# Rotary embedding on one core: tile 0 in one load with the tables behind it, and loads 5 to 7 issued together after store 2

## The chip, the cores and the metric

The kernel runs on one core of a Trainium2 chip. The metric is the device time of one execution in microseconds, lower being better. A run's profile gives the span from the first to the last instruction; the execution's time is a little longer than this.

The core has five engines with queues of their own: PE (matrix products; PEld is its weight load), DVE and POOL (elementwise work), ACT (here used to copy results out of PSUM) and SP, which in this kernel issues every transfer between main memory and the on-chip memory. The transfers themselves are carried by 16 DMA engines. PSUM is the small memory that matrix products write to.

## The reference

```python
# x (16, 512, 1024) float32; cos, sin (512, 32) float32; num_heads 16
x = x.reshape(batch, seq, num_heads, head_dim)           # head_dim 64
x1, x2 = x[..., :32], x[..., 32:]
rotated = concatenate([x1 * cos - x2 * sin, x1 * sin + x2 * cos], axis=-1)
```

cos and sin depend on the position in the sequence alone, and are the same for all batches and heads. 33.5 MB are read and 33.5 MB written; each element costs two products and one sum.

## The kernel before, in words

**Tiles.** The batch is cut into eight tiles of two batches each (`NB = 2`, `NT = 8`). A tile lies on 128 partitions, 64 for each of its batches; a partition holds eight consecutive positions of the sequence (`KK = 8`) of 1024 numbers each, 32 KB, which are contiguous in main memory. A tile is 4 MB. One of the eight positions of a tile is called a row here; the work is done row by row, on 128 x 1024 numbers.

**Buffers.** The pool `xp` has five tile buffers (`BUFS = 5`). The result of a tile is written over its input, so that one buffer is loaded, computed in place, stored from, and can be loaded again only when its store has landed. Tiles 5, 6 and 7 use the buffers of tiles 0, 1 and 2. The pool `bp` has six buffers of one row (`B_BUFS = 6`) for POOL's products; the raw sin and cos tables are first loaded into two of them. Three PSUM buffers `ps` of one row hold the sums.

**Tables.** sin and cos (64 KB each) are loaded on 64 partitions, spread to 128 by PE (lines 104 and 105), and DVE then makes the signed table `sns` from sin (lines 107 and 108) and copies a piece of it to PSUM (line 111). POOL's first product needs `sns`, DVE's first product the cos table in PSUM.

**A row.** POOL multiplies the row, with the halves of each head swapped, by `sns` into `b` (line 155), in all rows but row 6. DVE multiplies the row by cos into `ps` (line 156). For rows 1, 4 and 6 (`PE_ROWS`), PE adds the swapped product to `ps` by a product with the identity (line 164), and ACT copies the sum back over the row (line 167). For the other rows DVE adds the two (line 145). In row 6 DVE makes the swapped product itself, in place (line 158).

**Order.** The schedule is written out by hand: each engine runs its instructions in the order of the program, and waits where the data or a buffer is not there yet. SP's queue is in the same order. SP issues the first two rows of tile 0, then sin and cos, then the rest of tile 0 in pieces of two rows (`FIRST = (2, 4, 6, 8)`, four pieces of 1 MB, each with 8 KB a partition), then tiles 1 to 4 whole (32 KB a partition). In the loop over tiles, SP issues the store of tile t when its last row is computed (line 76); the last tile is stored in two halves (`LAST_OUT`). After the stores of tiles 1, 2 and 3 it issues load 5, 6 and 7 respectively (line 72 by way of line 180): so load 5 follows store 1, load 6 store 2 and load 7 store 3. Load 5 waits on SP until store 0 has landed, load 6 until store 1, load 7 until store 2. Whatever stands behind a waiting transfer on SP's queue waits too.

Of the kernel before, what the change touches and what calls it, by code (L numbers as in the profile page):

```python
# [13 lines left out]
BUFS = 5  # L14
# [4 lines left out]

DVE_B = (6,)  # L20

FIRST = (2, 4, 6, 8)
LAST_OUT = (4, 8)


# [1 line left out]
def kernel(  # L27
# [21 lines left out]
    NT = batch // NB  # L49
# [18 lines left out]
    def load(t, lo=0, hi=KK):  # L68
        if tiles[t] is None:
            tiles[t] = xp.tile([P, F], FP32, name="xt")  # L70
        s = slice(lo * dim, hi * dim)
        nc.sync.dma_start(out=tiles[t][:, s], in_=x_v[t][:, s])  # L72

    def store(t, lo=0, hi=KK):
        s = slice(lo * dim, hi * dim)
        nc.sync.dma_start(out=out_v[t][:, s], in_=tiles[t][:, s])

    load(0, 0, FIRST[0])
    sin_sb = bp.tile([P, dim], FP32, name="b")[:PB, : KK * half]
    cos_sb = bp.tile([P, dim], FP32, name="b")[:PB, : KK * half]  # L80
    nc.sync.dma_start(out=sin_sb, in_=sin_v)
    nc.sync.dma_start(out=cos_sb, in_=cos_v)
    for lo, hi in zip(FIRST, FIRST[1:]):
        load(0, lo, hi)
# [28 lines left out]
    def cos_b(k):  # L113
        c = cos_t[:, k * half : (k + 1) * half]
        return bass.AP(tensor=c.tensor, offset=c.offset, ap=[c.ap[0], [0, 2 * nh], [1, half]])

    def over_heads(s):
        return bass.AP(tensor=s.tensor, offset=s.offset, ap=[s.ap[0], [0, nh], [1, hd]])

    def swapped(r, n):  # L120
        return bass.AP(
            tensor=r.tensor, offset=r.offset + half, ap=[r.ap[0], [hd, n], [-half, 2], [1, half]]
        )

    def swapped_signed(i):

        s = sns_t[:, i * hd : (i + 1) * hd]
        return bass.AP(
            tensor=s.tensor, offset=s.offset + half, ap=[s.ap[0], [0, nh], [-half, 2], [1, half]]
        )  # L130

    def pairs(r):
        return r.rearrange("p (a j) -> p a j", j=half)
# [4 lines left out]
    def halves(r):  # L138
        return r.rearrange("p (h a j) -> p h a j", a=2, j=half)
# [3 lines left out]
    def add():  # L143
        r, ps, b = pending.pop(0)
        nc.vector.tensor_tensor(out=r, in0=ps, in1=b, op=ALU.add)  # L145

    for t in range(NT):
        xt = tiles[t]
        for k in range(KK):
            r = xt[:, k * dim : (k + 1) * dim]  # L150
            ps = pr.tile([P, dim], FP32, name="ps")
            if k not in DVE_B:
                b = bp.tile([P, dim], FP32, name="b")
                sk = sns[:, k].rearrange("p a j -> p (a j)")
                nc.gpsimd.tensor_tensor(out=halves(b), in0=swapped(r, nh), in1=over_heads(sk), op=ALU.mult)  # L155
            nc.vector.tensor_tensor(out=pairs(ps), in0=pairs(r), in1=cos_b(k), op=ALU.mult)  # L156
            if k in DVE_B:
                nc.vector.tensor_tensor(  # L158
                    out=halves(r), in0=halves(r), in1=swapped_signed(DVE_B.index(k)), op=ALU.mult
                )  # L160
            if k in PE_ROWS:
                for c in range(0, dim, BANK):
                    rhs = swapped(r[:, c : c + BANK], BANK // hd) if k in DVE_B else b[:, c : c + BANK]
                    nc.tensor.matmul(  # L164
                        out=ps[:, c : c + BANK], lhsT=ident, rhs=rhs, start=False, stop=True, skip_group_check=True
                    )
                nc.scalar.copy(out=r, in_=ps)  # L167
            else:
                pending.append((r, ps, b))
            while len(pending) > (1 if k + 1 < KK else 0):  # L170
                add()
        if t < NT - 1:
            store(t)
        else:
            lo = 0
            for hi in LAST_OUT:
                store(t, lo, hi)
                lo = hi
        if t >= 1 and t + BUFS - 1 < NT:
            load(t + BUFS - 1)  # L180


# [33 lines left out]
```

## Time and profile before

| | us |
|---|---|
| median of 8 runs | 165.05 |
| lowest and highest of them | 163.71 and 165.37 |
| the profiled execution's own time | 163.71 |
| its span | 161.8 |
| DVE busy | 132.5 |
| POOL busy | 130.2 |
| PE busy | 85.9 |
| ACT busy | 25.6 |

Over the span the transfers move 67.26 MB, 416 GB/s on average. How to read the page: busy time is that of an engine's instructions; the slices cut the span in 40 equal parts and give the busy share of each in tenths, for DMA the mean over its 16 engines. In a timeline the first column is the start of a piece in us from the span's start, the second its length, then the engine, the line and the operation, what it writes and reads, and how many were merged. An SP line of a transfer is its issue; the time from there to its landing is asked separately.

| transfers | count | KB each | median us from issue to landing |
|---|---|---|---|
| loads of a whole tile | 7 | 4096 | 29.3 |
| stores of a whole tile | 7 | 4096 | 26.1 |
| pieces of tile 0 | 4 | 1024 | 7.5 |
| halves of the last store | 2 | 2048 | 12.8 |
| sin, cos | 1 each | 64 | 4.9, 4.6 |

### The profile page before, as it was taken

How to read it: one execution, taken by the hardware profiler on the slowest of the kernel's cores; microseconds unless marked ns; L12 is line 12 of the kernel's file. 1: busy time of each engine (PE TensorE's matmuls, PEld its weight loads, DVE VectorE, ACT ScalarE, POOL GpSimd, SP SyncE). 2: the span in 40 equal slices, each digit the busy share in tenths (PEclk: the TensorE clock that was granted, in tenths of full speed). 3: DMA queues.
4: the chain of work that ended last, by engine and by line, in shares of the span. 5: the costliest groups of instructions: out<-in, count | busy, mean ns of one | idle time of the engine just before them, and what ended most of it. 6: DMA issues, size and time to landing. Idle time of an engine off the chain costs nothing.

```text
span 161.8 us, 602 instructions
## 1 busy us (share of the span) xinstructions
PE 85.9 (53%) x106; PEld 27.2 (17%) x106; DVE 132.5 (82%) x118; ACT 25.6 (16%) x25; POOL 130.2 (80%) x62
## 2 busy tenths in 40 slices
PE   6405380763785288328732773857584628472000
PEld 1202020221221022102210220222022202220000
DVE  1097656999999999999999999999999999997000
ACT  0000502102211211220222022012202220222000
POOL 1079999999999999999999999999999999300000
PEclk9999959675558555955589555555555895579655
DMA  5999999999999999999999999999999999999992
GB/s 186 389 421 462 421 478 397 413 486 397 413 486 389 397 470 429 399 478 413 405 478 413 413 462 423 389 486 421 397 437 446 405 462 429 405 462 397 425 437 109
DMA packets 3042, 67.26 MB, mean 416 GB/s; under 512 B 352, under 2 KB 480, under 8 KB 480
## 3 DMA queue, kind: packets, MB, share of 16 engines
q1 hardware_dynamic: 3040, 67.24, 97.5%
q14 instruction: 2, 0.02, 0.0%
HBM read 33.69 MB, written 33.55 MB: 416 GB/s over the span
## 4 chain that ended last, share of the span: by engine, by line
DVE 51%; PE 15%; issue 10%; POOL 6%; ACT 4%; DMA 3%; DVEq 1%; SPq 0%; ACTq 0%; POOLq 0%
DVE ps L156 30%; DVE xt L145 16%; PE ps L164 14%; POOL b L155 6%; DVE xt L158 5%; ACT xt L167 4%; DMA b<-in_sin_dram 3%; DVEq L211 1%; PE tab L104 1%; PE tab L105 1%; DVE sns L107 0%; SPq L72 0%; DVE sns L108 0%; DVEq L156 0%; DVEq L145 0%
## 5 line engine op out<-in xcount | busy, mean ns | idle before, releaser
L155 POOL TENSOR_TENSOR b<-xt,sns 128x1024 f32<-128x1024 f32 x56 | 129.5, 2347 | 8.1 <-DVE sns L108 7.8
L156 DVE TENSOR_TENSOR ps<-xt,tab 128x1024 f32<-128x1024 f32 x64 | 76.8, 1226 | 7.1 <-ACT xt L167 6.1
L164 PE MATMUL ps<-b,ident 128*128 128x512 f32 x64 | 54.9, 1007 | 46.8 <-DVE ps L156 31.7
L145 DVE TENSOR_TENSOR xt<-ps,b 128x1024 f32<-128x1024 f32 x40 | 48.0, 1217 | 0.9 <-POOL b L155 0.9
L167 ACT COPY xt<-ps 128x1024 f32<-128x1024 f32 x24 | 24.3, 1012 | 104.6 <-PE ps L164 95.2
L164 PE MATMUL ps<-xt,ident 128*128 128x512 f32 x32 | 26.3, 969 | 10.6 <-DVE xt L158 6.9
L164 PEld LDWEIGHTS ps<-b,ident 128*128 128x128 f32 x64 | 16.9, 290 | 83.2 <-issue 51.5
L164 PEld LDWEIGHTS ps<-xt,ident 128*128 128x128 f32 x32 | 8.4, 290 | 30.0 <-DVE xt L158 17.5
L158 DVE TENSOR_TENSOR xt<-xt,tab 128x1024 f32<-128x1024 f32 x8 | 9.8, 1220 | 0.3
L107 DVE TENSOR_SCALAR sns<-tab 128x256 f32<-128x256 f32 x1 | 0.4, 425 | 6.6 <-PE tab L105 6.6
L167 ACT ACT_TABLE_LOAD x1 | 1.3, 1283 | 17.6 <-PE ps L164 17.6
L95 PE MATMUL ps<-zero 128*128 128x512 bf16 x6 | 2.7, 630 | 1.2 <-DVE zero L89 1.2
L104 PE MATMUL tab<-b,spread 64*128 64x256 f32 x2 | 1.2, 696 | 2.2 <-DMA b<-in_sin_dram 2.2
L95 PEld LDWEIGHTS <-zero 128*128 128x128 bf16 x6 | 0.7, 137 | 2.3 <-DVE zero L89 1.2
L105 PE MATMUL tab<-b,spread 64*128 64x256 f32 x2 | 1.1, 631 | 0.0
L104 PEld LDWEIGHTS tab<-b,spread 64*128 64x128 f32 x2 | 0.5, 307 | 3.1 <-issue 3.1
L89 DVE MEMSET zero<- 128x256 uint32 x1 | 0.3, 272 | 0.9 <-PEq L197 0.9
L105 PEld LDWEIGHTS tab<-b,spread 64*128 64x128 f32 x2 | 0.7, 333 | 0.2
L103 DVE COPY spread<-ident 64x64 f32<-64x64 f32 x2 | 0.3, 181 | 0.2 <-POOL ident masks.py:199 0.2
masks.py:197 POOL MEMSET ident<- 128x128 f32 x1 | 0.2, 204 | 0.3 <-POOLq L197 0.3
L108 DVE COPY sns<-tab 128x256 f32<-128x256 f32 x1 | 0.4, 415 | 0.0
masks.py:199 POOL TENSOR_SCALAR_AFFINE_SELECT ident<-ident 128x128 f32<-128x128 f32 x1 | 0.3, 292 | 0.1
(5 smaller groups left out, 0.6 us busy)
## 6 DMA issues: line engine op xcount, KB each, us to landing
xt<-in_x_dram SPq DMA_DIRECT2D x7, 4096.0 KB, 29.3
out_dram<-xt SPq DMA_DIRECT2D x7, 4096.0 KB, 26.1
xt<-in_x_dram SPq DMA_DIRECT2D x4, 1024.0 KB, 7.5
out_dram<-xt SPq DMA_DIRECT2D x2, 2048.0 KB, 12.8
b<-in_sin_dram SPq DMA_DIRECT2D x1, 64.0 KB, 4.9
b<-in_cos_dram SPq DMA_DIRECT2D x1, 64.0 KB, 4.6
```

What stands on the lines that cost most here:

```text
L95: nc.tensor.matmul(out=ps[:, c : c + BANK], lhsT=zero[:, :P], rhs=zero, start=True, stop=True)
L104: nc.tensor.matmul(out=sin_t, lhsT=spread, rhs=sin_sb, start=True, stop=True)
L105: nc.tensor.matmul(out=cos_t, lhsT=spread, rhs=cos_sb, start=True, stop=True)
L107: nc.vector.tensor_scalar_mul(out=sns[:, :, 0, :], in0=sin_k, scalar1=-1.0)
L108: nc.vector.tensor_copy(out=sns[:, :, 1, :], in_=sin_k)
L145: nc.vector.tensor_tensor(out=r, in0=ps, in1=b, op=ALU.add)
L155: nc.gpsimd.tensor_tensor(out=halves(b), in0=swapped(r, nh), in1=over_heads(sk), op=ALU.mult)
L156: nc.vector.tensor_tensor(out=pairs(ps), in0=pairs(r), in1=cos_b(k), op=ALU.mult)
L158: nc.vector.tensor_tensor(out=halves(r), in0=halves(r), in1=swapped_signed(DVE_B.index(k)), op=ALU.mult)
L164: nc.tensor.matmul(out=ps[:, c : c + BANK], lhsT=ident, rhs=rhs, start=False, stop=True, skip_group_check=True)
L167: nc.scalar.copy(out=r, in_=ps)
L211: with _tile.TileContext(nc) as tc:
```

## The change

```diff
-FIRST = (2, 4, 6, 8)
+FIRST = (8,)
 LAST_OUT = (4, 8)
@@
-        if t >= 1 and t + BUFS - 1 < NT:
-            load(t + BUFS - 1)
+        if t + 1 == NT - BUFS:
+            for n in range(BUFS, NT):
+                load(n)
```

The first edit makes tile 0 one transfer of 4 MB with 32 KB a partition. The code around it stays, `load(0, 0, FIRST[0])` ahead of the two tables and a loop over the remaining pieces behind them, which is now empty. SP's queue therefore begins with the whole of tile 0, then sin, cos, and tiles 1 to 4.

The second edit acts once, at t = 2: after store 2, SP issues loads 5, 6 and 7 one behind the other. The order on SP's queue is then store 0, store 1, store 2, load 5, load 6, load 7, store 3 and so on to store 7. What each load waits for (stores 0, 1 and 2) is the same as before. No instruction on PE, DVE, ACT or POOL is added, removed or moved.

## The prediction

> **What bounds the kernel now.** I read the page's slices and DMA totals first, since a kernel that moves 67 MB for three operations on each element is likely bound by its transfers.
>
> ```profile
> span 161.8 us, 602 instructions
> ...
> DMA  5999999999999999999999999999999999999992
> ...
> q1 hardware_dynamic: 3040, 67.24, 97.5%
> ```
>
> Between the first and the last slice the transfer engines are full: there is no hole. One queue, SP's, carries all of it. So the time is the transfers' bytes at their rate, plus a head and a tail, as long as SP always has the next transfer queued before the last one is through. That condition is what I check next, in the order of time on SP's queue.
>
> ```profile
> 0.73 0.37 SPq L72 DMA_DIRECT2D xt<-in_x_dram  x1
> 1.16 0.53 SPq L81 DMA_DIRECT2D b<-in_sin_dram  x1
> 1.74 0.58 SPq L82 DMA_DIRECT2D b<-in_cos_dram  x1
> 2.36 4.35 SPq L72 DMA_DIRECT2D xt<-in_x_dram  x7
> 32.61 16.87 SPq L76 DMA_DIRECT2D out_dram<-xt  x2
> 62.86 0.34 SPq L72 DMA_DIRECT2D xt<-in_x_dram  x1
> 65.97 0.33 SPq L76 DMA_DIRECT2D out_dram<-xt  x1
> 72.67 0.34 SPq L72 DMA_DIRECT2D xt<-in_x_dram  x1
> 82.80 0.33 SPq L76 DMA_DIRECT2D out_dram<-xt  x1
> 92.10 0.34 SPq L72 DMA_DIRECT2D xt<-in_x_dram  x1
> ```
>
> The reader is to see when each transfer is handed over (first column). The store of tile 0 goes out at 32.61, that of tile 1 at 49.14, that of tile 2 at 65.97; load 5 at 62.86, the moment store 0 has landed (its issue-to-landing time, asked alone, is 30.2, so 62.8), and load 6 at 72.67, when store 1 has landed (49.14 + 23.5 = 72.6). With the issue-to-landing time of each transfer asked one by one, the landings stand in a row: tile 0's four pieces at 5.8, 8.9, 11.4, 13.9; loads 1 to 4 at 23.6, 33.3, 43.0, 53.0; then store 0 62.8, store 1 72.6, load 5 82.3, store 2 92.0, load 6 101.9, the rest one after another to 160.6. Each 4 MB tile takes 9.7 to 10.2. When store 1 ends at 72.6, load 5 has waited since 62.9 and store 2 since 66.0: nine and six us of reserve.
>
> Where compute begins is set by the tables:
>
> ```profile
> 6.17 1.19 PE L104 MATMUL tab<-b,spread 64*128 64x256 f32 x2 [2.24 <-DMA b<-in_sin_dram]
> 7.16 1.06 PE L105 MATMUL tab<-b,spread 64*128 64x256 f32 x2
> 8.25 0.42 DVE L107 TENSOR_SCALAR sns<-tab 128x256 f32<-128x256 f32 x1 [6.63 <-PE tab L105]
> 8.59 0.41 DVE L108 COPY sns<-tab 128x256 f32<-128x256 f32 x1
> 9.09 2.35 POOL L155 TENSOR_TENSOR b<-xt,sns 128x1024 f32<-128x1024 f32 x1 [7.79 <-DVE sns L108]
> ```
>
> sin lands at 6.04 (1.16 + 4.88 in the chain of waits), and POOL's first product starts at 9.09: 3.05 later, all of it the chain through PE and DVE. From there POOL never waits for x again:
>
> ```profile
> L155 POOL TENSOR_TENSOR b<-xt,sns x56: 2334/2347/2369, 9.1 to 136.5; 128x1024 f32<-128x1024 f32 x56
> ...
>   DVE sns L108: 7.8, 1
> ```
>
> Its 56 products start 2.31 apart (127.4 over 55 steps); the one real wait is that for the tables. In tile 0 the rows are wanted at 9.1, 13.7, 18.3 and 23.0 in pairs and their pieces land at 5.8, 8.9, 11.4 and 13.9, so none of the pieces is late. The stores of tiles 0 to 4 go out 16.5 to 16.8 apart, set by DVE (14 operations of 1.14 to 1.25 a tile), 23.5 after POOL's start for the first. Compute is thus a rigid train: if its start moves by D, every store's issue moves by D.
>
> **What the Trainium skill says.** "DMA: Bandwidth & Descriptors", section Queues, rings and completion order: each DMA engine consumes the descriptors of a ring in ring order. The trace agrees as far as it goes: sin, issued behind the first 1 MB piece, lands 0.28 after it, at 6.04 against 5.76. The same page, section Latency and other measured facts, gives about 0.6 us to the first byte of such a transfer; here the first one is issued at 0.73 and the first packets show at 1.74, so I use the measured 1.0. "TensorE: Matmul & The Clock Gate", Part 1: an idle window of about 3.4 us puts the clock back to half. PE idles longer before the tables after the change; but the four table matmuls already start 0.43 apart, and 256 columns in float32 at L164's later pace (0.85 for 512 in stretches granted half clock) are the same 0.43. They run at half clock now, so there is no warmth to lose.
>
> **The change part by part.**
>
> *Tile 0 in one transfer, the tables behind it.* Three issues fall away. Packets of 8 KB took 0.309 to 0.319 us in the trace, those of 32 KB mostly 1.213, which is 0.303 for 8 KB. Each engine carries 32 of the small ones, so 32 x about 0.008 = 0.25 saved. The bytes of tile 0 and the tables are the same, and in before they are all landed at 13.9; now at 13.6. But the tables come last: cos at 13.6, sin 0.33 ahead of it (the two lie 0.33 apart in before) at 13.3 instead of 6.0. So D = 13.3 - 6.04 = 7.25. cos lies no later behind sin than before, and its matmuls follow sin's. The chain of 3.05 stays: POOL starts at 16.3. All of tile 0 is there by then, but no row of it was waited for before, so this gives nothing back. Loads 1 to 4 land 0.25 earlier, and are wanted 7.25 later. The stores now go out at 39.9, 56.4 and 73.2.
>
> *Loads 5, 6 and 7 behind store 2.* On SP's queue they stood behind stores 1, 2 and 3; now the order is store 0, store 1, store 2, loads 5, 6, 7, store 3. Load 5 no longer goes out at 62.9 but only after SP has finished its wait for tile 2's compute, at 73.2. Stores 0 and 1 land at 62.5 and 72.35 (before, less 0.25). From there to 73.2 nothing is queued at all: DMA stands still. The two parts meet here. With the old start, store 2 would be issued at 66.0, 6.4 ahead, and its reserve would cover; D of 7.25 eats that.
>
> *The hole.* Store 2 issued at 73.2, first packets 1.0 later at 74.2, its 4 MB in 9.7 and about 0.35 from the last packet's end to the landing (the last store of before: 160.30 and 160.63): landed at 84.3, against 72.35 + 9.75 = 82.1 without a hole: 2.2. What is not shown is how fast a store starts into idle engines. The one start shown, the first 1 MB piece, had packets of up to 1.04 in place of 0.31 and cost slow engines some 1.2. Bounds 0 and 1.2; I take 0.2, since the stretch at the head also holds the very first accesses of the run, which the later one does not. Hole: 2.4.
>
> *After the hole.* Loads 5 and 6 are issued straight behind store 2 (stores 0 and 1 have landed), 19.4 of transfers. Load 7 waits on SP for store 2 (84.5), with store 3 behind it; tile 3 is computed at 90.0, so nothing real is held up, and DMA has work to 104. Load 5 lands at 84.5 + 9.7 = 94.2; POOL wants tile 5 at 89.92 + 7.25 = 97.2: 3 us of cover, where before there were 7.6 (82.3 to 89.9). Load 6 at 104 against 113.4, load 7 at 114 against 129.6. The turn of direction: tiles whose successor is of the other kind took 10.03 (load 4), 9.90 (load 6), 10.18 (load 7), but 9.68 (load 5); loads 5 and 6 are now followed by loads. Bounds 0 and 0.5; I take 0.2 saved.
>
> *Sum.* Last landing: 160.63 - 0.25 + 2.4 - 0.2 = 162.6. Against that stands compute's own tail: the last store is issued at 148.55 + 7.25 = 155.8, and alone it would take 1.0 + 4.85 + 0.35, landing at 162.0. That is earlier, so the transfers still end last, by 0.6 only: before, that reserve was 5.9 (148.55 + 6.2 = 154.7). The span grows by 1.95 to about 163.8. The profiled execution took 163.71 for its span of 161.8, 1.9 around it; after, 165.65 on its scale. The median of the runs is 165.05, 1.3 above the profiled one, so I add the 1.95 there: **167.0**.
>
> **The rivals.**
>
> *A, the forecast:* the hole before store 2 decides; 166.0 to 168.4. It would be shorter if tile 2's end came earlier. Row 6's four matmuls run at half clock there (3.79 in the chain of waits, but 1.98 in the last tile at full clock), which could bring the store forward or back by up to 1 us. For it: every number but the restart is in the trace. Chance 0.63.
>
> *B, no hole or one that is paid for:* store 2 comes 1.8 earlier through PE's clock and a faster start (0.6 of hole), and the turns save 0.5, with 0.25 from the packets: 165.05 - 0.15 = 164.9, no change. Against it: that needs all at their better bound. Chance 0.14.
>
> *C, the other side:* the tables do not come behind tile 0. If the small transfers overtake the 32 KB packets, as they would if an engine interleaved transfers instead of finishing them in order, sin lands near 6, D is about 0, store 2 is queued at 66 and only the savings stay: 0.25 + 0.5 and up to 0.5 of the head, 163.9. It decides if sin lands before about 11, for then the hole closes. Against it: sin landed after the piece ahead of it in before, not together with it. Chance 0.05.
>
> *D, a second wait behind the first:* DMA restarts slowly (1.2), and load 5 then lands at 95.2 and beyond; or the last store is late, if D is 8.5 and more, because then compute's tail rules, 148.55 + 8.5 + 6.2 = 163.3 and more, plus the slow start of its own. 3.2 to 4 in all: 168.3 to 169. Against it: 3 us of cover at load 5. Chance 0.18.
>
> **How the numbers follow.** The likeliest case gives 167.0. B's upper half and C lie under 165.4, D's far end over 168.8; 165.4 to 168.8 leaves out about 0.2. Half a per cent, 0.8 us, is about what a measurement of this kernel can tell from no change. Faster: C and a little of B, 0.05. The same: the rest of B and the low edge of A, 0.13. Slower: 0.82.
>
> **What would show it.** Right: sin and cos landing at 13 to 14, POOL's first product near 16.3, then 2.31 a row with no further wait; stores issued near 39.9, 56.4, 73.2; the GB/s of one slice near 73 clearly down; loads 5 and 6 issued within 1 us of store 2 and load 7 near 84.5; the last store issued near 155.8. Wrong: a full DMA row around 73, or POOL starting near 9, would refute the hole and D; a hole as told with an unchanged time would mean that the transfers gained elsewhere as much; idle time on POOL before tile 5 would be D's sign.

## The result and the profile after

The changed kernel takes 167.01 us (median of 11 runs, 166.48 to 167.85), against 164.83 of the kernel before beside it (32 runs): ratio 1.0132, 95% interval 1.0111 to 1.0153. It is slower, by 2.2 us. Runs that count as slow (over 1.5% above the fastest of their kernel) are left out of the ratios, here and below, so that a ratio need not be the quotient of the two medians. The profiled execution took 166.67 for a span of 164.6. The kernel before was profiled in the fastest of its runs, 163.71, so the two profiles lie 3.0 apart, 0.8 more than the medians.

The page of after, slices and DMA total:

```profile
span 164.6 us, 594 instructions
...
DMA  7899989989999899958898989989999989989896
...
q1 hardware_dynamic: 2608, 67.24, 96.6%
```

The bytes are those of before. The row of nines now has a 5 in its 18th slice (from 70.0 to 74.1 us).

SP's queue of after in order of time (start, length up to the last issue, what, how many):

```profile
2.35 2.10 SPq L72 DMA_DIRECT2D xt<-in_x_dram  x4
40.54 32.86 SPq L76 DMA_DIRECT2D out_dram<-xt  x3
73.57 12.00 SPq L72 DMA_DIRECT2D xt<-in_x_dram  x3
89.90 67.66 SPq L76 DMA_DIRECT2D out_dram<-xt  x6
```

Stores 0, 1 and 2 are now one group (issued at 40.54, 55.44 and 73.07), and the loads one group behind it. Store 1 has landed at 71.9, 1.1 before store 2 is issued. Load 5 was free to go from 62.3, when store 0 landed, but stands behind store 2 until 73.57.

The start of compute in after:

```profile
13.67 1.19 PE L104 MATMUL tab<-b,spread 64*128 64x256 f32 x2 [9.75 <-DMA b<-in_sin_dram]
14.66 1.06 PE L105 MATMUL tab<-b,spread 64*128 64x256 f32 x2
15.76 0.42 DVE L107 TENSOR_SCALAR sns<-tab 128x256 f32<-128x256 f32 x1 [14.14 <-PE tab L105]
16.10 0.42 DVE L108 COPY sns<-tab 128x256 f32<-128x256 f32 x1
16.59 2.34 POOL L155 TENSOR_TENSOR b<-xt,sns 128x1024 f32<-128x1024 f32 x1 [15.30 <-DVE sns L108]
```

The same steps in the same lengths, 7.5 later: sin lands at 13.54, 0.30 behind tile 0 (13.24), and the chain from there to POOL is 3.05 again. The matmuls start 0.43 apart as they did.

The hole, busy time of each engine by stretches of time (the last two columns are the share of DMA and GB/s):

```profile
72.30:73.80 1.50, 0.00 (x0) 0.00 (x0) 1.29 (x2) 0.74 (x1) 1.50 (x1) 1.00 0.00 0
73.80:85.20 11.40, 7.03 (x9) 2.16 (x9) 11.05 (x10) 2.02 (x2) 11.40 (x6) 0.56 1.05 414
85.20:94.90 9.70, 6.50 (x8) 1.83 (x8) 9.59 (x9) 1.68 (x3) 9.70 (x5) 0.68 1.00 432
```

In this 1.5 us stretch no byte moves, while POOL is busy all the time and DVE nearly so: the transfers wait for compute to hand over tile 2. Store 2 lands at 85.16, 13.24 behind store 1; in the kernel before it landed 9.75 behind the transfer ahead of it.

The end of after, in order of time:

```profile
156.19 1.01 ACT L167 COPY xt<-ps 128x1024 f32<-128x1024 f32 x1 [3.66 <-PE ps L164]
157.23 0.33 SPq L76 DMA_DIRECT2D out_dram<-xt  x1
```

The last store is issued at 157.23, 8.7 later than before, and lands 6.3 after that. Before, it stood behind other stores for most of its 12.1. In after, too, the store ahead of it is still on its way when it is issued: that one lands at 158.70, and the last one 4.84 behind it.

### The profile page after: what moved, and what is told of

It reads as the page before. It is cut to its first block, busy times and chain, and to the rows that moved or that the text cites. A ratio compares the mean times of both kernels' runs of the same rounds, so it can differ in the third digit from the quotient of the medians.

```text
span 164.6 us, 594 instructions
## 1 busy us (share of the span) xinstructions
PE 85.2 (52%) x106; PEld 26.5 (16%) x106; DVE 132.5 (81%) x118; ACT 25.6 (16%) x25; POOL 130.1 (79%) x62
## 4 chain that ended last, share of the span: by engine, by line
DVE 49%; PE 18%; issue 10%; DMA 8%; ACT 5%; POOL 5%; POOLq 0%; DVEq 0%; ACTq 0%
DVE ps L156 29%; PE ps L164 18%; DVE xt L145 15%; DMA xt<-in_x_dram 8%; DVE xt L158 6%; ACT xt L167 5%; POOL b L155 5%; POOLq L155 0%; DVEq L156 0%; ACTq L167 0%
## 5 line engine op out<-in xcount | busy, mean ns | idle before, releaser
L155 POOL TENSOR_TENSOR b<-xt,sns 128x1024 f32<-128x1024 f32 x56 | 129.4, 2377 | 15.6 <-DVE sns L108 15.3
L164 PE MATMUL ps<-b,ident 128*128 128x512 f32 x64 | 52.2, 964 | 48.2 <-DVE ps L156 34.5
L164 PE MATMUL ps<-xt,ident 128*128 128x512 f32 x32 | 28.3, 1034 | 11.8 <-DVE xt L158 8.1
L164 PEld LDWEIGHTS ps<-b,ident 128*128 128x128 f32 x64 | 15.7, 270 | 83.0 <-issue 43.0
L164 PEld LDWEIGHTS ps<-xt,ident 128*128 128x128 f32 x32 | 8.9, 307 | 32.0 <-DVE xt L158 19.0
## 6 DMA issues: line engine op xcount, KB each, us to landing
b<-in_sin_dram SPq DMA_DIRECT2D x1, 64.0 KB, 12.4
b<-in_cos_dram SPq DMA_DIRECT2D x1, 64.0 KB, 12.1
```

What stands on the lines that cost most here:

```text
L164: nc.tensor.matmul(out=ps[:, c : c + BANK], lhsT=ident, rhs=rhs, start=False, stop=True, skip_group_check=True)
```

## The experiments

Ratios are to the kernel before, run beside each; the medians of before were 164.67, 164.70 and 164.74 in the three sets.

The theory: a late start of compute opens two places that can each set the end, the hole before store 2 and a last store that starts when the queue is empty. The rivals: the hole alone costs the time; or the single first transfer does by itself.

A caution for the traces: each is of one run. Those of the kernel before, of the packets alone, of load 5 ahead of store 2 and of seven rows ahead of the tables are of runs 0.7 to 1.1 below their medians, that of the tables first of one 1.15 above. What the other runs do differently is not in a trace.

### The packets alone

```diff
-FIRST = (2, 4, 6, 8)
+FIRST = (8,)
```

(against before)

> Tile 0 in one transfer with the tables behind it, but loads 5, 6, 7 behind stores 1, 2, 3 as before. Theory (two limits lie close together: the hole before store 2, and compute's late tail): load 5 is issued near 62.4, so DMA has no hole near 73; but POOL still starts near 16.6, the last store is still issued near 157, meets idle DMA engines and needs about 7 more, so the execution stays 1.3 to 2.2 us above before (166.1 to 167.0). Rival (the hole alone is the cost): without it the time is that of before, 164.6 to 165.0.

Measured: 166.07, ratio 1.0083 (1.0050 to 1.0117), 1.40 above before. SP's queue of this kernel:

```profile
62.67 0.34 SPq L72 DMA_DIRECT2D xt<-in_x_dram  x1
73.57 0.33 SPq L76 DMA_DIRECT2D out_dram<-xt  x1
```

Load 5 is back at 62.67 and covers the time to store 2, so there is no hole, and yet over half the loss stays. The busy time by stretches at the end shows where:

```profile
150.00:156.80 6.80, 3.46 (x6) 0.68 (x4) 5.81 (x5) 2.02 (x2) 0.00 (x0) 0.90 0.74 313
156.90:162.40 5.50, 0.00 (x0) 0.00 (x0) 0.00 (x0) 0.00 (x0) 0.00 (x0) 0.62 0.90 381
```

Before the last store DMA is 0.74 busy and moves 313 GB/s: engines stand idle. The store, issued at 156.16, lands 6.3 later, its 16 engines within 0.2 of each other; the store ahead of it had landed between 156.01 and 157.35, one engine late. The rival "the hole alone" falls.

### The order of the loads alone

```diff
-FIRST = (8,)
+FIRST = (2, 4, 6, 8)
```

(against after)

> Tile 0 in four pieces with the tables behind the first, as before; loads 5, 6, 7 together behind store 2, as after. Theory: compute starts near 9.1, store 2 is issued near 66, more than 5 us ahead of store 1's landing near 72.4, so no hole; fewer turns from loads to stores save 0 to 0.5: 164.3 to 164.9. Rival (the grouping of the loads costs by itself, for instance through load 7's wait for store 2 on SP): 166 or more.

Measured: 163.51, ratio 0.9930 (0.9906 to 0.9954), 1.16 faster than before, more than expected; why it gains so much stays open (see the kernel before once more). SP's queue here:

```profile
33.14 32.25 SPq L76 DMA_DIRECT2D out_dram<-xt  x3
65.49 17.61 SPq L72 DMA_DIRECT2D xt<-in_x_dram  x3
```

Store 2 is issued at 65.05, store 1 lands at 73.0: eight us in reserve, no hole. Load 5 lands at 92.35, later than POOL wants tile 5; POOL waits 2.5 for it, and the last store goes out at 149.81 in place of 148.55, which the queue of stores still hides. So the two edits do not add: +1.40 and -1.16 alone, +2.2 together. With an early start the grouping gains; with a late one it costs 0.9 (166.07 against 167.01).

### The tables first

```diff
-    load(0, 0, FIRST[0])
@@
     nc.sync.dma_start(out=cos_sb, in_=cos_v)
+    load(0, 0, FIRST[0])
```

(against after)

> As after, but sin and cos are issued ahead of tile 0's one transfer. Theory: the tables land near 3.5, tile 0 near 13.8, and this now starts POOL, so D is about 4.8 and store 2 is issued near 70.8, with 0.8 to the first packet: a hole of 0 to 0.8, the last store issued near 154 and not the limit: 164.3 to 165.2. Rival (a single first transfer costs in itself, wherever the tables are): 166.5 to 167.2 as after.

Measured: 164.98, ratio 1.0031 (1.0003 to 1.0059). POOL now waits for tile 0 itself and starts at 14.5, 2.1 earlier than in after:

```profile
L155 POOL TENSOR_TENSOR b<-xt,sns x56: 2343/2357/2376, 14.5 to 142.1; 128x1024 f32<-128x1024 f32 x56
...
  DMA xt<-in_x_dram: 13.2, 1
```

Store 2 is issued at 71.20. It has 2.9 us in reserve in this trace, but store 1 lands at 74.07 there, 2.1 later than in after (load 4 took 10.62, store 1 10.19); had it landed as in after, the reserve would be 0.7. Two us come back by moving 128 KB ahead of 4 MB, so the rival as it was put, after's loss wherever the tables are, falls. The single transfer is still not free: with the same order of loads and tile 0 in pieces the time was 163.51, 1.5 less, and POOL started 5.3 earlier, since it did not have to wait for all of tile 0.

### Two pieces, the tables behind the first

```diff
-FIRST = (8,)
+FIRST = (2, 8)
```

(against after)

> Loads 5 to 7 together behind store 2; tile 0 in two transfers, two rows, then the tables, then six rows. Theory: compute starts near 9.1; the second piece lands near 13.7, when row 2 is wanted, so POOL waits 0 to 0.4; no hole; 164.2 to 164.8. Rival (pieces of tile 0 that land just in time stall the rows): 165.5 or more.

Measured: 163.82, ratio 0.9944 (0.9925 to 0.9964). Compute starts at 9.6. Six rows in one piece instead of in three make no difference that can be told from the kernel with four pieces (0.9930).

### Load 5 ahead of store 2

```diff
-        if t + 1 == NT - BUFS:
-            for n in range(BUFS, NT):
-                load(n)
+        if t == 1:
+            load(5)
+        if t == 2:
+            load(6)
+            load(7)
```

(against after)

> As after, but load 5 is issued behind store 1 (as before), and loads 6 and 7 behind store 2. Theory: load 5 goes out near 62.4 and covers the time to store 2 near 73, so there is no hole; compute's late tail stays, the last store issued near 156.5 and landed 6.3 later: 165.3 to 166.3, below after's 167.0. Rival (after's loss is in the single first transfer, not in the hole): 166.8 to 167.3.

Measured: 166.41, ratio 1.0129 (1.0080 to 1.0178), a little above the expected range; by the ratios it cannot be told from after (1.0132).

```profile
62.73 0.34 SPq L72 DMA_DIRECT2D xt<-in_x_dram  x1
71.97 0.33 SPq L76 DMA_DIRECT2D out_dram<-xt  x1
```

Load 5 goes out at 62.73 and the hole is gone; the last store is issued at 156.29 and lands 6.3 later, all engines within 0.2, while the transfer ahead of it had landed at 156.15. With the hole closed, the tail sets the end in this trace: the last store lands 6.45 behind the one ahead, where 4.84 is usual.

### A shorter tail, without and with the hole

```diff
-LAST_OUT = (4, 8)
+LAST_OUT = (4, 6, 8)
```

once on the kernel with the packets alone, once on after.

> As e1_packets_only (tile 0 in one transfer, tables behind it, loads 5 to 7 as before), with the last tile stored in three pieces, rows 0 to 3, 4 and 5, 6 and 7. Theory: in e1 the last 2 MB store started into idle engines and set the end; with 1 MB left the tail is 2.4 shorter and the queue of transfers sets it: 164.5 to 165.5, against 166.07 of e1. Rival (e1's loss lies in slow packets at its head and turns): 165.8 to 166.3, as e1.

> As after, with the last tile stored in three pieces, rows 0 to 3, 4 and 5, 6 and 7. Theory: after the hole the queue of transfers and compute's tail end within 0.5 of each other, so a shorter tail alone brings 0 to 0.6: 166.4 to 167.0. Rival (compute's tail alone sets the end in after too): 164.6 to 165.3.

Measured without the hole: 164.94, ratio 1.0038 (1.0015 to 1.0061), against 1.0083 with two halves. The end of it in order of time:

```profile
155.04 2.56 SPq L76 DMA_DIRECT2D out_dram<-xt  x2
156.23 1.01 ACT L167 COPY xt<-ps 128x1024 f32<-128x1024 f32 x1 [3.66 <-PE ps L164]
```

The last issue, at 157.27, is 1.1 later than with two halves, but its 1 MB takes 4.5 to land instead of 6.3. Store 6, issued at 140.43, was late too: the first engine had ended store 5 at 139.3, and 15 of the 16 finished store 6 within 0.2 of each other, so most engines had run dry before it as well. Measured with the hole: 167.46, ratio 1.0195 (1.0146 to 1.0244): above the expected range, and nothing gained. The hole stands in its stretches as in after:

```profile
72.30:73.70 1.40, 0.41 (x1) 0.00 (x0) 1.40 (x2) 0.95 (x1) 1.40 (x2) 1.00 0.00 0
```

And the stores are still queued when the last one comes: it is issued at 157.89, and the one ahead lands at 162.17.

Closing the hole alone gains 0.9 us (the packets alone, 1.0083) or nothing sure (load 5 ahead, 1.0129), shortening the tail alone nothing (1.0195); both together bring the kernel to 1.0038. That is the mark of two limits side by side.

### How late is too late

```diff
-FIRST = (8,)
+FIRST = (6, 8)
```

(against after, and once with (7, 8))

> As after, but tile 0 in two transfers: six rows, then the tables, then two rows. Theory (the hole and the tail open only beyond a delay of the start of some 5 to 6 us): sin lands near 11.2, POOL starts near 14.2, store 2 is issued near 71.1, about 1 ahead of store 1's landing, so the engines hardly stand still, and the last store, issued near 154, does not set the end: 163.6 to 164.6. Rival (the time follows the delay of the start in proportion, 163.5 at no delay and 167.0 at 7.5): 165.7 to 166.2.

> As after, but tile 0 in two transfers: seven rows, then the tables, then one row. Theory: sin lands near 12.3, store 2 is issued near 72.2, about when store 1 lands, with 0.8 to its first packets: store 2's landing 10.5 to 12.5 behind store 1's, in place of 13.2 in after, and 164.8 to 166.4. Rival (in proportion to the delay): 166.1 to 166.6.

POOL's products of these two (count, shortest, median and longest in ns, first and last start), the first with six rows ahead of the tables:

```profile
L155 POOL TENSOR_TENSOR b<-xt,sns x56: 2332/2348/2378, 14.3 to 141.6; 128x1024 f32<-128x1024 f32 x56
```

and with seven:

```profile
L155 POOL TENSOR_TENSOR b<-xt,sns x56: 2332/2348/2373, 15.3 to 142.4; 128x1024 f32<-128x1024 f32 x56
```

| rows ahead of the tables | sin lands | POOL starts | store 2 issued | store 1 lands | store 2 behind store 1 | median us | ratio |
|---|---|---|---|---|---|---|---|
| 2 (four pieces) | 6.13 | 9.2 | 65.05 | 73.0 | 9.7 | 163.51 | 0.9930 |
| 6 | 11.21 | 14.3 | 69.94 | 72.3 | 10.1 | 164.95 | 1.0014 |
| 7 | 12.27 | 15.3 | 70.52 | 72.1 | 10.5 | 165.76 | 1.0064 |
| 8 (after) | 13.54 | 16.6 | 73.07 | 71.9 | 13.2 | 167.01 | 1.0132 |

With seven rows the result is in the expected range; with six it is 0.35 above it. The first 5 us of delay cost 1.4, the next 2.3 cost 2.1: bent, as a reserve that runs out, but not flat before the bend, and both kernels below what the proportional rival said. The tables-first kernel, whose POOL starts at 14.5, took 164.98, as the six-row kernel with 14.3: the time goes with the start of compute, not with the size of tile 0's pieces. What the six-row kernel loses is not a hole. Its store 2 was queued 2.3 ahead, yet load 5 took 10.66 and load 7 10.30 in place of 9.7, with single packets of up to 2.57 us where 1.213 is usual.

### The kernel before once more

> The kernel before, unchanged, for a second profile of it. Each turn from loads to stores (loads 4, 5, 6 and 7) costs between 0 and 0.6 again, 0.8 to 1.8 in all, more than the 0.6 of e2_rounds_only's two turns; time 164.0 to 165.5.

Measured: 163.82 in one run, 0.18 below the expected range. Loads 4 to 7 took 10.35, 9.79, 9.81 and 10.06, 1.17 above four times 9.71, against 0.95 in the first profile. In the kernel with the order of the loads alone the same four took 10.07, 9.66, 9.71 and 10.30: 0.90. The turns into stores thus do not show the 1.16 that it gains by its median. That profile is of the slowest of its runs (163.99), and those of before are at the low end of theirs, so single profiles do not settle where the gain lies.

## Why the prediction was right

It said 167.0, range 165.4 to 168.8, slower; measured 167.01. The mechanism held step by step: the tables late, compute late as a whole, a hole before store 2. The agreement to 0.01 is luck. The prediction added 1.95 to a median of 165.05; beside after, the kernel before took 164.83, and the difference is 2.18. Between the two profiles the last landing moved by 2.92 (160.63 to 163.55), and there three terms come out otherwise than put in: -0.7 for -0.25 ahead of the hole, 3.5 for 2.4 in it, 0.1 for -0.2 behind it.

**The delay of the start.** Predicted 7.25, measured 7.5. The tables came behind tile 0, 0.30 after it; rival C (they overtake it) fell. "DMA: Bandwidth & Descriptors", section Queues, rings and completion order, in the Trainium skill says that an engine consumes a ring in order; the trace agrees with a table that waited 12.4 us for its 64 KB. The four table matmuls kept their pace of 0.43; the profile's clock row shows full clock there in both kernels, so that the half clock of the prediction rests on the pace alone.

**The packets' saving.** Predicted 0.25 by the time tile 0 and both tables are in; measured nothing: 13.85, against 13.87 and, in the second profile of before, 13.55. The 32 KB packets of the first wave (the first packet on each engine) took up to 2.2 us each in place of 1.213, which gave the saving back. Further on more was gained than predicted: load 1, load 4 and store 1 took 9.56, 9.72 and 9.65 in place of 9.72, 10.02 and 9.81, so that store 1 landed 0.68 earlier, at 71.92 against 72.60. Why is not known.

**The train.** Stores predicted at 39.9, 56.4 and 73.2, measured at 40.54, 55.44 and 73.07. POOL ran on from 16.59 without a wait for data; load 5 landed at 94.9, ahead of POOL's need at 97.4. Rival D's wait for load 5 did not come.

**The hole.** Predicted 2.4, measured 13.24 - 9.75 = 3.5. The first packets came 0.83 after the issue, earlier than the 1.0 that was put in, and the start was hardly slow (1.24 and 1.26 a packet in the first two waves, 0.08 in all, where 0.2 was put in). Some 1.1 came at the end of the transfer, at the turn from store 2 to load 5: the last 16 packets of store 2, which started at 82.5 to 82.6, took 1.93 on average. The prediction had no such term.

Two things suggest that the length of the hole goes with PE's clock, as rival A had noted. In the kernel with load 5 ahead of store 2, compute starts 0.36 later than in after, but the clock granted from 66 to 73 us is 0.95 against 0.59, and store 2 goes out at 71.97 against 73.07. And of the eleven runs of after, the four with a mean granted clock under 0.66 took 167.16 to 167.85, the seven with 0.738 or more 166.48 to 167.15; the 44 runs of before beside the packets alone show no such order (median 164.53 under 0.7, 164.78 above). That is a correlation, not an experiment.

**The turns.** Predicted 0.2 saved behind the hole; not seen: loads 5, 6 and 7 took 9.73, 9.71 and 10.41 in after, 9.68, 9.90 and 10.19 before. The order of the loads alone is worth 1.16 by its median, but with an early start.

**The tail.** Predicted to land 0.6 ahead of the transfers, with 6.2 from issue to landing; measured 6.3, and the last store at 157.23 where 155.8 was said. The delay gives 0.25 of that. The rest, 1.2, fits PE's clock, granted at 0.50 from 153 to 158: row 6's product made ACT wait 3.66 in the last tile of after, and 1.86 before, as this line of the kernel before, in order of time, shows:

```profile
146.82 1.01 ACT L167 COPY xt<-ps 128x1024 f32<-128x1024 f32 x1 [1.86 <-PE ps L164]
```

The packets-alone kernel, which starts 0.4 later than after but waited 1.86 there, issued its last store at 156.16. In after, tail and queue ended level: the store ahead landed at 158.15 on the first engine and 158.70 on the last, and the last store's own packets were due 0.83 after 157.23, at 158.06. Rival B (the hole is paid for) fell with the measured 2.2 us. What the prediction had as a check, compute's tail close below, proved to be a second limit, which sets the end once the hole is closed.

**Open.** Packets at the turn behind store 2 were slower in the kernels where store 2 was queued late: between 79 and 84 us they cost an engine next to nothing more than the usual 1.213 each with 8 us of reserve, about 0.3 with 2.9 us, 0.9 with 2.3 us, and 0.7 in after (1.0 up to 86). This was seen and not explained. It was not tried whether keeping the engines busy through the hole with other bytes removes it. Nor is it known where the order of the loads alone gains its 1.16.

## What to carry to other kernels

A transfer-bound kernel has its reserve in the queue: for each transfer, compare its issue with the landing of the one ahead of it. The last store needs such a reserve as well. Small inputs that start compute belong ahead of large ones: here 64 KB behind 4 MB moved the whole train by 7.5 us. The first piece of work should not wait for more bytes than it needs, either: with the tables first, the whole tile 0 still held compute until 14.5. Grouping loads into fewer rounds gained 0.7% here with four pieces of tile 0, and with a late start its sign turned, so the two must be judged together. The version to keep is the order of the loads alone, at 163.51, faster than both kernels.

## What the hardware showed unexpectedly

A 2 MB store issued into idle engines needed 6.3 us to its landing, 4.85 of it for the bytes at the usual rate; the first packets came 0.83 after the issue. Larger packets at the head gained nothing: the first wave of 32 KB packets took up to 2.2 us each. In the three kernels with tile 0 whole and load 5 issued early, one of the 16 engines was 1.4 to 2.2 us behind the next one when load 5 landed (in the packets-alone kernel 83.97 against 81.78), and in that kernel still 2.3 behind when store 5 landed, 59 us later.
